# A two-layer fp32 trunk on one core: other places and turns for weights, a norm's root ahead of its queue, later dots, and one halved output at the end

## The chip, the cores and the metric

The kernel runs on one core of a Trainium2 chip. The metric is the device time of one execution in microseconds (us); the value of a kernel is the median of its runs.

## What is computed

The input is x with 512 tokens of 1024 features and a vector c; all numbers are fp32. Two layers follow each other, each with a mixer and an MLP, and each of the four parts begins with a norm whose scale, shift and gate come from c:

```python
for layer in range(2):
    mod = silu(c) @ ada_w[layer] + ada_b[layer]
    shift1, scale1, gate1, shift2, scale2, gate2 = split(mod, 6)
    h = rms_norm(x, norm_mix[layer]) * (1 + scale1) + shift1
    x = x + gate1 * mixer(h)          # layer 0: convolution and HGRN2; layer 1: stick-breaking attention
    h = rms_norm(x, norm_mlp[layer]) * (1 + scale2) + shift2
    x = x + gate2 * (square(relu(h @ w1[layer])) @ w2[layer])
```

## The kernel before

**Products.** TensorE (PE) holds a 128x128 piece of a weight and streams 512 or 256 tokens past it. For fp32 accuracy each weight and each activation is split into a high half and a rest, and `mm3` issues three matmuls for a product: L281 (high weight, high activation), L282 (high weight, low activation), L283 (low weight, high activation). A tile of weights is 128x1024. Its way is: a load from memory by SyncE's queue (L260, tile `wraw`, a ring of three), a cast on ScalarE (ACT) that makes the high half (L271, `whi`), a subtraction on VectorE (DVE) that makes the rest (L272, `wlo`). `whi` and `wlo` are rings of four, so a cast waits until PE has finished with the tile four turns earlier; a tile can also be given a place of its own (`of`), outside the ring. Tiles of the graph (below) go the same way with L1370, L1372 and L1373.

**Layer 0.** The functions are called in program order, and each engine takes its instructions in that order. The out projection (`proj`) makes eight outputs; outputs 4 to 7 (`HALVED`) are computed in two halves of 256 tokens, first half first, and `PLACES` says which of them have a weight place of their own. After each output `x_add` (L505) adds it to x, and the norm sums squares (`nsq`, `nss`). When a half is complete, L496 on PE sums over features, ACT and DVE make the root (`na`, `ny`), and per feature tile DVE makes `tt` (L465), ACT `hh` (L466) and DVE `hl` (L467). Then the MLP: `mlp_head` makes four hidden tiles half by half with the weights w1[0] to w1[3]; two whole tiles follow (w1[4], w1[5]); all others come in pairs by a Strassen-like scheme (`pair`), which needs sums of activations (`sums`, tiles t0 to t3) and of weights (`pair_w`). Four blocks `b` of eight hidden tiles each are multiplied with w2 (`second`, `products`). The function `rest()` is the end of a block's last pair: its hidden tile is split into `hidh` (L290, ACT) and `hidl` (L291, DVE), and the next product waits for it.

**Dots.** The 96 products of c with the weights of scale, shift and gate of both layers are done on DVE, 80 of them in `background(n)`: each loads 128x1024 weights into the same raw ring and multiplies and sums them (L419). `PIECES[b][o]` says how many stand behind output o of block b.

**Layer 1.** Up to its MLP's first four hidden tiles it is a graph of operations that a planner orders: each operation has an engine, a cost, what it reads and writes, and a priority (the number behind the lists in `on_act` and `on_dve`; the lower number goes first among those that are ready). PE's order is partly fixed as a chain. `finish` (L1400 to L1421) is the graph's norm: L1406 sums on PE, L1409 and L1410 make the logarithm and the exponential on ACT, L1411 to L1413 polish the root on DVE, and L1417, L1419 and L1421 make `tt`, `hh` and `hl` per feature tile. Attention begins with queries and keys of the first heads, whose squares (`nsq`, L1433 and L1450) PE sums by L1459. After the graph `mlp(1, True, ...)` runs in program order on PE, with the other engines in the same way, and at the end the outputs that are left are computed half by half, added to x and stored.

Of the kernel before, what the change touches and what calls it, by code (L numbers as in the profile page):

```python
# [13 lines left out]
F32 = mybir.dt.float32  # L14
# [5 lines left out]
AF = mybir.ActivationFunctionType  # L20
ALU = mybir.AluOpType
# [5 lines left out]
EPS = 1e-6  # L27
# [193 lines left out]
def trunk(tc, x_d, c_d, rep_d, small_d, const_d, ada_d, ws_d, win_d, wv_d, woab_d, w1_d, w2_d, wqk_d, wvc_d, woc_d, out_d):  # L221
# [30 lines left out]
    H = halves()  # L252
# [251 lines left out]
    def x_add(o, ps, sl, l, v):  # L504
        dve.scalar_tensor_tensor(x[o][:, sl], ps, mcol(l, v, o), x[o][:, sl], op0=ALU.mult, op1=ALU.add)  # L505
# [463 lines left out]
            nrm.add(o, sl)  # L969

    HALVED = (4, 5, 6, 7)
    PLACES = {5: (mp, "F2", "Q2"), 6: (mp, "Ft", "Kt")}
    w = [load_w(woab_d[o]) for o in (0, 1, 2)]
    background(2)
    run(proj((0, 1, 2), w, FULL))
# [161 lines left out]

    PIECES = ((2, 2, 3, 2, 2, 2), (2, 2, 3, 2, 2, 2), (2, 2, 2, 2, 2, 2), (2, 2, 2, 2, 2))  # L1140

    def mlp(l, last, hp, head, th, more=()):

        nrm = Norm(1, 0, (7,)) if not last else None
        ahead = None
        for b in range(4):
            hid, rest = list(head) if b == 0 else [], lambda: None
            if b == 0:
                for n, j in enumerate((4, 5)):
                    whole_tile(more[n] if more else load_w(w1_d[l, j]), j, hp, hid)  # L1150
            for i in range(len(hid) // 2, 4):
                rest = pair(4 * b + i, hp, th, hid, rest, ahead or pair_w(l, 4 * b + i, hp))
                ahead = None
            n = 8 if b < 3 else 5
            second = lambda o: (acc(), load_w(w2_d[l, b // 2, o, b % 2], None, AT256 if o == n - 1 else AT512))

            def products(p, k0, k1):
                for k in range(k0, k1):
                    mm3(p[0], p[1], ks(k), hid[k], FULL, k == 0, k == 7)

            def done(o, ps):
                x_add(o, ps, FULL, l, GATE2)
                if b == 3:
                    if last:
                        sync.dma_start(out_d[o], x[o])
                    else:
                        nrm.add(o, FULL)
                if 0 < o < len(PIECES[b]):
                    background(PIECES[b][o])

            p0 = second(0)
            products(p0, 0, 7)
            rest()
            background(PIECES[b][0])
            p1 = second(1)
            products(p1, 0, 7)
            for o, p in enumerate((p0, p1)):
                products(p, 7, 8)
                done(o, p[0])
            for o in range(2, n):  # L1180
                p = p1 if o == n - 1 and b < 3 else second(o)
                if o == n - 2 and b < 3:

                    p1, ahead = second(n - 1), pair_w(l, 4 * b + 4, hp)
                    next(ahead)
                    next(ahead)
                products(p, 0, 8)
                done(o, p[0])
# [12 lines left out]
        return nrm, ps, banks, hid, ws

    def mlp_head(l, nin, hp):
# [109 lines left out]
    def on_act(n, fn, r, w, prio=1, psum=False, column=False, **kw):  # L1313
        return G.op("ACT", act_us(n, psum, column), fn, r, w, prio, **kw)

    def on_dve(n, fn, r, w, prio=1, **kw):
        return G.op("DVE", dve_us(n), fn, r, w, prio, **kw)
# [83 lines left out]
    def finish(parts, hf, l, which, table, after=()):  # L1401

        sl, ps, a, y = H[hf], miscs.new(), nass.new(), nys.new()

        for i, q in enumerate(parts):
            on_pe(0.44, lambda i=i, q=q: pe.matmul(ps.t[:, :256], ones, q.t[:, sl], start=(i == 0), stop=(i == len(parts) - 1)),  # L1406
                  (q,), (ps,), 0, after=after if i == 0 else ())
        m = lambda: ps.t[:, :256]
        on_act(256, lambda: act.activation(a.t, m(), AF.Ln, scale=LS, bias=eps_b), (ps,), (a,), 0, psum=True, column=True, after=table)  # L1409
        on_act(256, lambda: act.activation(y.t, a.t, AF.Exp, scale=-0.5, bias=ls_b), (a,), (y,), 0, column=True)  # L1410
        on_dve(256, lambda: dve.scalar_tensor_tensor(a.t, m(), EPS, y.t, op0=ALU.add, op1=ALU.mult), (ps, y), (a,), 0)  # L1411
        on_dve(256, lambda: dve.tensor_tensor(a.t, a.t, y.t, op=ALU.mult), (y, a), (a,), 0)
        on_dve(256, lambda: dve.scalar_tensor_tensor(y.t, a.t, -3.0, y.t, op0=ALU.add, op1=ALU.mult), (a, y), (y,), 0)  # L1413
        for i in range(NT):
            t_, g, sh = tth[i][hf], l * 16 + which * 8 + i, mcol(l, SHIFT1 if which == 0 else SHIFT2, i)
            hi, lo = hh[hf][i]
            on_dve(310, lambda i=i, t_=t_, g=g: dve.scalar_tensor_tensor(t_.t[:, sl], x[i][:, sl], gsc[:, g:g + 1], y.t,  # L1417
                   op0=ALU.mult, op1=ALU.mult), (xh[i, hf], y), (t_,), 0)
            on_act(256, lambda t_=t_, sh=sh, hi=hi: act.activation(hi.t[:, sl], t_.t[:, sl], AF.Identity, bias=sh), (t_,), (hi,), 0,  # L1419
                   column=True)  # L1420
            on_dve(310, lambda t_=t_, sh=sh, hi=hi, lo=lo: dve.scalar_tensor_tensor(lo.t[:, sl], t_.t[:, sl], sh,  # L1421
                   hi.t[:, sl].bitcast(F32), op0=ALU.add, op1=ALU.subtract), (t_, hi), (lo,), 0)


    QQ, KK, kraw, sqs, rq, oT, vs = {}, {}, {}, {}, {}, {}, {}
# [277 lines left out]
    for hf, sl in enumerate(H):  # L1703
        if hf:
            finish([nt_.acc[1]] + [nt_.sq[o, 1] for o in nt_.direct], 1, 1, 1, (), [order[at + 8]])

        ps = [accs.new() for _ in range(2)] if hf == 0 else [zts.new() for _ in range(4)]
        ps = [(ps[j // 2], lambda t_, j=j: t_[:, H[j % 2]]) if hf == 0 else (ps[j], half) for j in range(4)]

        for k, j in by_half(0, 4) if hf == 0 else [(k, j) for js in ((0, 1), (2, 3)) for k in range(NT) for j in js]:  # L1710
            order.append(mm3h(*ps[j], w[j], ks(k), (hh[hf][k],), sl, k == 0 and (hf == 1 or j % 2 == 0), k == NT - 1, 256))
        for j in range(4):
            c_, (hi, lo), (p_, cut) = cms.new(), hid[j], ps[j]
            on_act(256, lambda c_=c_, p_=p_, cut=cut, sl=sl: act.activation(c_.t[:, sl], cut(p_.t), AF.Relu), (p_,), (c_,), 0, psum=True)
# [9 lines left out]
    order_s.close()  # L1724
    order_s.enter_context(tc.manual_schedule(engines={mybir.EngineType.PE}))

    _, ps, _, hk, ws = mlp(1, True, h1, [(a.t, b.t) for a, b in hid], [(a.t, b.t) for a, b in th])
    for hf in range(2):
        for o in range(5, 8):
            for k in range(8):  # L1730
                mm3(ps[o, hf], ws[o - 5], ks(k), hk[k], H[hf], k == 0, k == 7)
            x_add(o, ps[o, hf], H[hf], 1, GATE2)
            sync.dma_start(out_d[o][:, H[hf]], x[o][:, H[hf]])
    order_s.close()
    m_s1.close()
    es.close()
# [69 lines left out]
```

## Time and profile before

| What | Value |
|---|---|
| median of 3 runs | 1243.63 us (1243.44, 1243.63, 1245.4) |
| the profiled execution | 1245.21 us, its span 1243.4 us |
| TensorE busy | 1217.4 us, 98% of the span |
| TensorE weight load busy | 1058.9 us, 85% |
| VectorE busy | 890.5 us, 72% |
| ScalarE busy | 618.7 us, 50% |
| mean granted TensorE clock | 0.996 of 2.4 GHz |

The span is the time between the first and the last instruction of the profiled execution; 1.8 us of that execution lie around it. An engine is busy while it executes an instruction; TensorE's matmuls overlap, so that its busy time holds their pipeline too. In the views below a time such as 268.60 is counted from the span's start, and a bracket at a row's end gives the idle time of that engine just before, with what ended it.

### The profile page before, as it was taken

How to read it: one execution, taken by the hardware profiler on the slowest of the kernel's cores; microseconds unless marked ns; L12 is line 12 of the kernel's file. 1: busy time of each engine (PE TensorE's matmuls, PEld its weight loads, DVE VectorE, ACT ScalarE, POOL GpSimd, SP SyncE). 2: the span in 40 equal slices, each digit the busy share in tenths (PEclk: the TensorE clock that was granted, in tenths of full speed). 3: DMA queues.
4: the chain of work that ended last, by engine and by line, in shares of the span. 5: the costliest groups of instructions: out<-in, count | busy, mean ns of one | idle time of the engine just before them, and what ended most of it. 6: DMA issues, size and time to landing. Idle time of an engine off the chain costs nothing.

```text
span 1243.4 us, 19173 instructions
## 1 busy us (share of the span) xinstructions
PE 1217.4 (98%) x7649; PEld 1058.9 (85%) x7649; DVE 890.5 (72%) x1435; ACT 618.7 (50%) x1111; POOL 11.2 (1%) x24
## 2 busy tenths in 40 slices
PE   7999999989999999999999999999989999999998
PEld 6888877889899899898977877787878898998998
DVE  8996868769788687787857765568694585665761
ACT  4433233347256265274568655667465283472650
POOL 0000000000000000000300000000000000000000
PEclk9999999999999999999999999999999999999999
DMA  8764444623745727527332122323114223143141
GB/s 305 258 208 161 143 153 135 203 69 107 246 135 183 245 92 244 179 99 259 110 102 85 52 68 85 94 60 103 35 37 134 85 101 122 58 146 102 54 151 51
DMA packets 46618, 163.50 MB, mean 131 GB/s; under 512 B 5296, under 2 KB 6328, under 8 KB 46528
## 3 DMA queue, kind: packets, MB, share of 16 engines
q1 hardware_dynamic: 46384, 161.78, 39.5%
q8 instruction: 60, 0.98, 0.3%
q10 hardware_dynamic: 144, 0.49, 0.1%
q14 instruction: 30, 0.25, 0.1%
HBM read 155.96 MB, written 2.10 MB: 127 GB/s over the span
## 4 chain that ended last, share of the span: by engine, by line
PE 84%; DVE 8%; DMA 4%; ACT 2%; issue 1%; SPq 0%; DVEq 0%; ACTq 0%
PE b L281 20%; PE b L283 20%; PE b L282 20%; PE acc L281 3%; PE acc L283 3%; PE acc L282 3%; PE b L1539 2%; PE b L1560 1%; DMA raw<-in_ws 1%; PE b L1595 1%; PE b L1459 1%; DMA wraw<-in_w 1%; PE b L1596 1%; PE b L1597 1%; DVE wlo L272 1%
## 5 line engine op out<-in xcount | busy, mean ns | idle before, releaser
L271 ACT CAST whi<-wraw 128x1024 fp32r<-128x1024 f32 x125 | 130.0, 1048 | 217.9 <-DMA wraw<-in_w 87.7
L282 PE MATMUL b<-hidl,whi 128*128 128x512 f32 (+1 forms) x560 | 208.4, 372 | 1.0 <-DVE hidl L291 1.0
L281 PE MATMUL b<-hidh,whi 128*128 128x512 f32 (+1 forms) x560 | 208.6, 373 | 0.2
L283 PE MATMUL b<-hidh,wlo 128*128 128x512 f32 (+1 forms) x560 | 208.0, 371 | 0.0
L283 PE MATMUL b<-hh,wlo 128*128 128x256 f32 (+1 forms) x632 | 193.5, 306 | 7.1 <-DVE wlo L272 7.1
L281 PE MATMUL b<-hh,whi 128*128 128x256 f32 (+1 forms) x632 | 197.6, 313 | 2.0 <-ACT hh L1419 2.0
L282 PE MATMUL b<-hl,whi 128*128 128x256 f32 (+1 forms) x632 | 193.3, 306 | 1.2 <-DVE hl L1421 1.2
L272 DVE TENSOR_TENSOR wlo<-wraw,whi 128x1024 fp32r<-128x1024 f32 x125 | 152.1, 1222 | 58.8 <-ACT whi L271 57.6
L281 PEld LDWEIGHTS b<-hh,whi 128*128 128x128 f32 x632 | 120.4, 191 | 14.6 <-issue 7.2
L283 PEld LDWEIGHTS b<-hh,wlo 128*128 128x128 f32 x632 | 120.5, 191 | 13.3 <-DVE wlo L272 7.8
L282 PEld LDWEIGHTS b<-hl,whi 128*128 128x128 f32 x632 | 121.8, 193 | 6.2 <-DVE hl L1421 1.8
L282 PEld LDWEIGHTS b<-hidl,whi 128*128 128x128 f32 x560 | 105.6, 188 | 19.5 <-DVE hidl L291 1.6
L505 DVE SCALAR_TENSOR_TENSOR x<-b,modc,x 128x512 f32<-128x512 f32 (+1 forms) x102 | 68.2, 675 | 75.2 <-PE b L283 75.1
L281 PEld LDWEIGHTS b<-hidh,whi 128*128 128x128 f32 x560 | 105.2, 188 | 19.1 <-ACT hidh L290 1.0
L283 PEld LDWEIGHTS b<-hidh,wlo 128*128 128x128 f32 x560 | 105.2, 188 | 18.5
L419 DVE CUSTOM_DVE_ANT_0 wraw<-wraw,cb 128x1024 f32<-128x1024 f32 x80 | 97.4, 1221 | 26.3 <-DMA wraw<-in_ada 25.9
L272 DVE TENSOR_TENSOR wlo<-tt,whi 128x1024 fp32r<-128x1024 f32 x52 | 63.4, 1221 | 22.5 <-ACT whi L271 21.9
L271 ACT CAST whi<-tt 128x1024 fp32r<-128x1024 f32 x52 | 53.4, 1049 | 45.3 <-PE b L282 32.7
L1373 DVE TENSOR_TENSOR wlo<-raw,whi 128x1024 fp32r<-128x1024 f32 x34 | 41.6, 1222 | 23.6 <-ACT whi L1372 23.5
L291 DVE TENSOR_TENSOR hidl<-cm,hidh 128x256 fp32r<-128x256 f32 (+1 forms) x90 | 44.4, 510 | 18.5 <-ACT hidh L290 17.7
L281 PE MATMUL acc<-hh,whi 128*128 128x512 f32 x128 | 52.3, 408 | 0.0
L1523 DVE TENSOR_TENSOR_SCAN om<-om,pat 128x772 f32<-128x772 f32 (+2 forms) x24 | 46.5, 1936 | 5.8 <-ACT om L1519 5.8
(378 smaller groups left out, 2631.4 us busy)
## 6 DMA issues: line engine op xcount, KB each, us to landing
wraw<-in_w SPq DMA_DIRECT2D x124, 512.0 KB, 3.6
wraw<-in_ada SPq DMA_DIRECT2D x80, 512.0 KB, 4.3
eraw<-in_ada SPq DMA_DIRECT2D x16, 512.0 KB, 3.7
wraw<-in_win SPq DMA_DIRECT2D x16, 512.0 KB, 3.5
raw<-in_wqk SPq DMA_DIRECT2D x16, 512.0 KB, 4.1
raw<-in_ws SPq DMA_DIRECT2D x8, 512.0 KB, 6.0
wraw<-in_woab SPq DMA_DIRECT2D x8, 512.0 KB, 3.2
raw<-in_wvc SPq DMA_DIRECT2D x8, 512.0 KB, 3.3
```

Source lines behind the costliest of these rows:

```text
L271: act.copy(hi, raw)
L272: dve.tensor_tensor(lo, raw, hi.bitcast(F32), op=ALU.subtract)
L281: pe.matmul(ps, whi, h[0][:, hs], start=start, stop=False, **kw)
L282: pe.matmul(ps, whi, h[1][:, hs], start=False, stop=False, **kw)
L283: pe.matmul(ps, wlo, h[0][:, hs], start=False, stop=stop, **kw)
L291: dve.tensor_tensor(lo[:, sl], t_[:, sl], hi[:, sl].bitcast(F32), op=ALU.subtract)
L419: dve.tensor_tensor_reduce(out=raw, in0=raw, in1=cb, scale=1.0, scalar=0.0, op0=ALU.mult, op1=ALU.add, accum_out=modr[:, col:col + 1])
L505: dve.scalar_tensor_tensor(x[o][:, sl], ps, mcol(l, v, o), x[o][:, sl], op0=ALU.mult, op1=ALU.add)
L1373: on_dve(1024, lambda: dve.tensor_tensor(lo.t, raw.t, hi.t.bitcast(F32), op=ALU.subtract), (raw, hi), (lo,), 1)
L1459: on_pe(0.13, lambda s=s, sq=sqs[p, s, s0]: pe.matmul(ms.t[64 + 32 * s:96 + 32 * s, sl], hs, sq.t[:, sl], start=True, stop=True), (sqs[p, ...
L1523: on_dve(2 * nw, lambda: dve.tensor_tensor_scan(s_(), s_(), pats[i][:, ::-1], 0.0, op0=ALU.mult, op1=ALU.max), (om,), (om,), 2)
L1539: pe.transpose(tp.t[:, o_:o_ + P], be.t[:, w0:w0 + P], ident)
```

## The change

- The out projection's outputs 6 and 7, and no longer 5 and 6, have weight places of their own.
- Behind output 0 of a block the dots no longer stand between `rest()` and `second(1)` but behind the output's end, like all others; the count behind output 0 is now 0, and the others take more.
- In the graph's norm the root's operations have priority -1 instead of 0, and `tt`, `hh`, `hl` of the second half of the tokens (`hf` is 1) have -1 too.
- The two whole tiles' weights of layer 1's MLP, w1[4] and w1[5], are loaded and split inside the graph, before the sums.
- At the end of layer 1 only output 7 is halved; outputs 5 and 6 are computed with 512 tokens like the others.

```diff
-    PLACES = {5: (mp, "F2", "Q2"), 6: (mp, "Ft", "Kt")}
+    PLACES = {6: (mp, "F2", "Q2"), 7: (mp, "Ft", "Kt")}
...
-    PIECES = ((2, 2, 3, 2, 2, 2), (2, 2, 3, 2, 2, 2), (2, 2, 2, 2, 2, 2), (2, 2, 2, 2, 2))
+    PIECES = ((0, 2, 3, 3, 3, 2), (0, 2, 3, 3, 3, 2), (0, 2, 3, 3, 2, 2), (0, 2, 3, 3, 2))
...
-            n = 8 if b < 3 else 5
+            n = 8 if b < 3 else 7 if last else 5
...
-                if 0 < o < len(PIECES[b]):
+                if o < len(PIECES[b]):
                     background(PIECES[b][o])
...
             rest()
-            background(PIECES[b][0])
             p1 = second(1)
...
-        on_act(256, lambda: act.activation(a.t, m(), AF.Ln, scale=LS, bias=eps_b), (ps,), (a,), 0, psum=True, column=True, after=table)
-        on_act(256, lambda: act.activation(y.t, a.t, AF.Exp, scale=-0.5, bias=ls_b), (a,), (y,), 0, column=True)
+        on_act(256, lambda: act.activation(a.t, m(), AF.Ln, scale=LS, bias=eps_b), (ps,), (a,), -1, psum=True, column=True, after=table)
+        on_act(256, lambda: act.activation(y.t, a.t, AF.Exp, scale=-0.5, bias=ls_b), (a,), (y,), -1, column=True)
...
             on_dve(310, lambda i=i, t_=t_, g=g: dve.scalar_tensor_tensor(t_.t[:, sl], x[i][:, sl], gsc[:, g:g + 1], y.t,
-                   op0=ALU.mult, op1=ALU.mult), (xh[i, hf], y), (t_,), 0)
+                   op0=ALU.mult, op1=ALU.mult), (xh[i, hf], y), (t_,), -hf)
...
+    more = [weights(w1_d[1, j]) for j in (4, 5)]
     sums(1, th, issue)
...
-    _, ps, _, hk, ws = mlp(1, True, h1, [(a.t, b.t) for a, b in hid], [(a.t, b.t) for a, b in th])
+    _, ps, _, hk, ws = mlp(1, True, h1, [(a.t, b.t) for a, b in hid], [(a.t, b.t) for a, b in th], [(a.t, b.t) for a, b in more])
...
-        for o in range(5, 8):
-            for k in range(8):
-                mm3(ps[o, hf], ws[o - 5], ks(k), hk[k], H[hf], k == 0, k == 7)
-            x_add(o, ps[o, hf], H[hf], 1, GATE2)
-            sync.dma_start(out_d[o][:, H[hf]], x[o][:, H[hf]])
+        for k in range(8):
+            mm3(ps[7, hf], ws[0], ks(k), hk[k], H[hf], k == 0, k == 7)
+        x_add(7, ps[7, hf], H[hf], 1, GATE2)
+        sync.dma_start(out_d[7][:, H[hf]], x[7][:, H[hf]])
```

PE's own order is the same in both kernels but for two places: the end, which has 48 matmuls fewer, and the start of layer 1's attention, where one L1459 stands three matmuls earlier. What moves is on the other engines, at three places.

**Place 1: DVE at the end of layer 0's out projection**, as a piece of the difference. `ny` is the root of the first half's norm, `tt` belongs to that norm, and `wlo` is the low half of w1[3].

```order
 L505 SCALAR_TENSOR_TENSOR x_66<-acc,modc,x_66 128x256
 L336 SCALAR_TENSOR_TENSOR ny<-na,ny 128x256
+L272 TENSOR_TENSOR wlo<-wraw,whi 128x1024
 L465 SCALAR_TENSOR_TENSOR tt<-x_61,gsc,ny 128x256
 L465 SCALAR_TENSOR_TENSOR tt<-x_62,gsc,ny 128x256
```

The same instruction stood before behind the eight `tt`, the eight `hl` and the last addition to x; it is now ahead of them, and its cast on ACT, too, stands ahead of the first `hh`.

**Place 2: ACT at the start of layer 1's attention**, the order of the change. `nsq<-b_5879` and `nsq<-b_5891` are the squares of the first two heads' queries, `nsq<-b_5884` those of the first keys, and `hh` is the norm's high half for the second half of the tokens.

```order
L1433 ACTIVATE nsq<-b_5879 128x256
L1419 ACTIVATE hh_5628<-tt,modc 128x256
L1419 ACTIVATE hh_5630<-tt,modc 128x256
L1419 ACTIVATE hh_5632<-tt,modc 128x256
L1419 ACTIVATE hh_5634<-tt,modc 128x256
L1437 CAST stq<-b_5879 64x256 x2
L1449 COPY kraw<-b_5884 128x256
L1450 ACTIVATE nsq<-b_5884 128x256
L1433 ACTIVATE nsq<-b_5891 128x256
```

Before, the four `hh` stood behind all the squares of the first two heads; on PE the three L1459 that read the squares of the first queries, the first keys and the second queries now stand in a row.

**Place 3: DVE at the end of the graph**, first before, then in the change. `t0l` to `t3l` are the low halves of the sums, L1717 makes `hidl` of the first four hidden tiles, and the first two of the three `wlo` belong to w1[4] and w1[5].

```order
L1026 TENSOR_TENSOR t0l<-tt,t0h 128x1024
L1033 SCALAR_TENSOR_TENSOR tt<-tt,modc 128x256 x5
L1717 TENSOR_TENSOR hidl_8954<-cm,hidh_8939 128x256
L1717 TENSOR_TENSOR hidl_8960<-cm,hidh_8944 128x256
L1033 SCALAR_TENSOR_TENSOR tt<-tt,modc 128x256 x3
L1026 TENSOR_TENSOR t1l<-tt,t1h 128x1024
L1026 TENSOR_TENSOR t2l<-tt,t2h 128x1024
L1026 TENSOR_TENSOR t3l<-tt,t3h 128x1024
L1717 TENSOR_TENSOR hidl_8981<-cm,hidh_8972 128x256
L1717 TENSOR_TENSOR hidl_8993<-cm,hidh_8983 128x256
L272 TENSOR_TENSOR wlo<-wraw,whi 128x1024 x3
```

```order
L1033 SCALAR_TENSOR_TENSOR tt<-tt,modc 128x256 x2
L1372 TENSOR_TENSOR wlo<-raw,whi 128x1024
L1033 SCALAR_TENSOR_TENSOR tt<-tt,modc 128x256
L1717 TENSOR_TENSOR hidl_8979<-cm,hidh_8966 128x256
L1372 TENSOR_TENSOR wlo<-raw,whi 128x1024
L1033 SCALAR_TENSOR_TENSOR tt<-tt,modc 128x256 x3
L272 TENSOR_TENSOR wlo<-wraw,whi 128x1024
L1717 TENSOR_TENSOR hidl_9012<-cm,hidh_8994 128x256
L1717 TENSOR_TENSOR hidl_9039<-cm,hidh_9025 128x256
L1033 SCALAR_TENSOR_TENSOR tt<-tt,modc 128x256 x2
L1026 TENSOR_TENSOR t1l<-tt,t1h 128x1024
L1026 TENSOR_TENSOR t2l<-tt,t2h 128x1024
```

All three `wlo` now stand ahead of `t1l` to `t3l`. A little earlier on DVE, three `hl` of the norm (L1421) have moved ahead of the sums' first subtraction (L1036), behind which they stood.

## Rows read from the trace of the kernel before

**Rows 1.** The page: busy times, a group of instructions, a kind of load.

```profile
PE 1217.4 (98%) x7649; PEld 1058.9 (85%) x7649; DVE 890.5 (72%) x1435; ACT 618.7 (50%) x1111; POOL 11.2 (1%) x24
...
L419 DVE CUSTOM_DVE_ANT_0 wraw<-wraw,cb 128x1024 f32<-128x1024 f32 x80 | 97.4, 1221 | 26.3 <-DMA wraw<-in_ada 25.9
...
wraw<-in_w SPq DMA_DIRECT2D x124, 512.0 KB, 3.6
```

**Rows 2.** Waits of PE over the span: total us, times, longest.

```profile
PE b L283 <- DVE wlo L272: 7.1, 2, 4.0
...
PE b L281 <- ACT hh L1419: 2.0, 1, 2.0
```

**Rows 3.** Timeline of PE around 268 us: start, us, instruction, idle before.

```profile
268.60 0.57 PE L283 MATMUL b<-hh,wlo 128*128 128x256 f32 x1 [3.19 <-DVE wlo L272]
...
271.52 0.86 PE L496 MATMUL b<-nss,ones 128*128 128x256 f32 x2
```

**Rows 4.** Timeline of PE, 889 to 925 us.

```profile
891.92 0.38 PE L281 MATMUL b<-hh,whi 128*128 128x256 f32 x1 [1.97 <-ACT hh L1419]
...
912.11 0.39 PE L282 MATMUL b<-hl,whi 128*128 128x256 f32 x1 [0.52 <-DVE hl L1421]
...
923.56 0.50 PE L283 MATMUL b<-hh,wlo 128*128 128x512 f32 x1 [3.96 <-DVE wlo L272]
```

**Rows 5.** Windows: length, busy us (x instructions) of PE, PEld, DVE, ACT, POOL, then granted clock, DMA.

```profile
893.28:896.70 3.42, 3.42 (x18) 3.42 (x17) 3.42 (x10) 1.71 (x4) 0.00 (x0) 0.50 0.00 0
924.00:927.42 3.42, 3.42 (x10) 2.67 (x9) 1.77 (x2) 0.00 (x0) 0.00 (x0) 0.50 0.69 216
...
268.64:272.06 3.42, 3.42 (x15) 3.33 (x16) 0.00 (x0) 0.00 (x0) 0.00 (x0) 0.50 0.46 153
```

**Rows 6.** Timeline of DVE, 259 to 269 us.

```profile
259.07 0.41 DVE L336 SCALAR_TENSOR_TENSOR ny<-na,ny 128x256 f32<-128x256 f32 x1
...
266.94 0.47 DVE L505 SCALAR_TENSOR_TENSOR x<-acc,modc,x 128x256 f32<-128x256 f32 x1
267.33 1.21 DVE L272 TENSOR_TENSOR wlo<-wraw,whi 128x1024 fp32r<-128x1024 f32 x1
```

**Rows 7.** Timeline of ACT, 263 to 268 us.

```profile
263.81 1.05 ACT L271 CAST whi<-wraw 128x1024 fp32r<-128x1024 f32 x1
...
267.50 0.42 ACT L485 ACTIVATE nsq<-x 128x256 f32<-128x256 f32 x1 [1.10 <-DVE x L505]
```

**Rows 8.** Timeline of PE in layer 0's MLP, last block.

```profile
567.51 0.50 PE L282 MATMUL b<-hidl,whi 128*128 128x512 f32 x1 [0.74 <-DVE hidl L291]
```

**Rows 9.** Timeline of ACT at the start of layer 1's attention.

```profile
622.50 0.39 ACT L1450 ACTIVATE nsq<-b 128x256 f32<-128x256 f32 x1
...
624.63 1.30 ACT L1419 ACTIVATE hh<-tt,modc 128x256 fp32r<-128x256 f32 x3
```

**Rows 10.** Timeline of PE at the start of layer 1's attention.

```profile
622.95 0.62 PE L1459 MATMUL b<-nsq,cons 128*32 128x256 f32 x2 [0.22 <-ACT nsq L1450]
```

**Rows 11.** Timeline of DVE, 889 to 935 us.

```profile
889.99 0.48 DVE L505 SCALAR_TENSOR_TENSOR x<-b,modc,x 128x256 f32<-128x256 f32 x1 [0.20 <-PE b L283]
890.39 0.41 DVE L1413 SCALAR_TENSOR_TENSOR ny<-na,ny 128x256 f32<-128x256 f32 x1
...
920.48 1.22 DVE L1026 TENSOR_TENSOR t3l<-tt,t3h 128x1024 fp32r<-128x1024 f32 x1
...
922.28 3.49 DVE L272 TENSOR_TENSOR wlo<-wraw,whi 128x1024 fp32r<-128x1024 f32 x3
928.74 0.69 DVE L1065 TENSOR_TENSOR tt<-wraw 128x512 f32<-128x512 f32 x1 [2.97 <-DMA wraw<-in_w]
...
931.76 2.49 DVE L272 TENSOR_TENSOR wlo<-tt,whi 128x1024 fp32r<-128x1024 f32 x2
```

**Rows 12.** Windows of PE alone at 512 and at 256 tokens: length, busy us (x matmuls), clock, DMA.

```profile
1203.00:1213.00 10.00, 10.00 (x45) 1.00 0.31 107
1228.00:1238.00 10.00, 10.00 (x87) 1.00 0.13 42
```

More of the change, by code (lines that the diff above doesn't have):

```diff
@@ L1194, in mlp @@
         ps, banks, ws = {}, {}, []
-        for o in range(5, 8):
+        for o in range(n, 8):
             for hf in range(2):
@@ L1198, in mlp @@
                 ps[o, hf] = acc(256)
-            ws.append(load_w(w2_d[l, 1, o, 1], None if o == 5 else (hp, f"t{o - 6}h", f"t{o - 6}l"), AT256))
+            ws.append(load_w(w2_d[l, 1, o, 1], None if o == n else (hp, f"t{o - 6}h", f"t{o - 6}l"), AT256))
         return nrm, ps, banks, hid, ws
@@ L1408, in finish @@
         m = lambda: ps.t[:, :256]
-        on_act(256, lambda: act.activation(a.t, m(), AF.Ln, scale=LS, bias=eps_b), (ps,), (a,), 0, psum=True, column=True, after=table)
-        on_act(256, lambda: act.activation(y.t, a.t, AF.Exp, scale=-0.5, bias=ls_b), (a,), (y,), 0, column=True)
-        on_dve(256, lambda: dve.scalar_tensor_tensor(a.t, m(), EPS, y.t, op0=ALU.add, op1=ALU.mult), (ps, y), (a,), 0)
-        on_dve(256, lambda: dve.tensor_tensor(a.t, a.t, y.t, op=ALU.mult), (y, a), (a,), 0)
-        on_dve(256, lambda: dve.scalar_tensor_tensor(y.t, a.t, -3.0, y.t, op0=ALU.add, op1=ALU.mult), (a, y), (y,), 0)
+        on_act(256, lambda: act.activation(a.t, m(), AF.Ln, scale=LS, bias=eps_b), (ps,), (a,), -1, psum=True, column=True, after=table)
+        on_act(256, lambda: act.activation(y.t, a.t, AF.Exp, scale=-0.5, bias=ls_b), (a,), (y,), -1, column=True)
+        on_dve(256, lambda: dve.scalar_tensor_tensor(a.t, m(), EPS, y.t, op0=ALU.add, op1=ALU.mult), (ps, y), (a,), -1)
+        on_dve(256, lambda: dve.tensor_tensor(a.t, a.t, y.t, op=ALU.mult), (y, a), (a,), -1)
+        on_dve(256, lambda: dve.scalar_tensor_tensor(y.t, a.t, -3.0, y.t, op0=ALU.add, op1=ALU.mult), (a, y), (y,), -1)
         for i in range(NT):
@@ L1417, in finish @@
             on_dve(310, lambda i=i, t_=t_, g=g: dve.scalar_tensor_tensor(t_.t[:, sl], x[i][:, sl], gsc[:, g:g + 1], y.t,
-                   op0=ALU.mult, op1=ALU.mult), (xh[i, hf], y), (t_,), 0)
-            on_act(256, lambda t_=t_, sh=sh, hi=hi: act.activation(hi.t[:, sl], t_.t[:, sl], AF.Identity, bias=sh), (t_,), (hi,), 0,
+                   op0=ALU.mult, op1=ALU.mult), (xh[i, hf], y), (t_,), -hf)
+            on_act(256, lambda t_=t_, sh=sh, hi=hi: act.activation(hi.t[:, sl], t_.t[:, sl], AF.Identity, bias=sh), (t_,), (hi,), -hf,
                    column=True)
             on_dve(310, lambda t_=t_, sh=sh, hi=hi, lo=lo: dve.scalar_tensor_tensor(lo.t[:, sl], t_.t[:, sl], sh,
-                   hi.t[:, sl].bitcast(F32), op0=ALU.add, op1=ALU.subtract), (t_, hi), (lo,), 0)
+                   hi.t[:, sl].bitcast(F32), op0=ALU.add, op1=ALU.subtract), (t_, hi), (lo,), -hf)
     QQ, KK, kraw, sqs, rq, oT, vs = {}, {}, {}, {}, {}, {}, {}
@@ L1725, in trunk @@
     order_s.enter_context(tc.manual_schedule(engines={mybir.EngineType.PE}))
-    _, ps, _, hk, ws = mlp(1, True, h1, [(a.t, b.t) for a, b in hid], [(a.t, b.t) for a, b in th])
+    _, ps, _, hk, ws = mlp(1, True, h1, [(a.t, b.t) for a, b in hid], [(a.t, b.t) for a, b in th], [(a.t, b.t) for a, b in more])
     for hf in range(2):
-        for o in range(5, 8):
-            for k in range(8):
-                mm3(ps[o, hf], ws[o - 5], ks(k), hk[k], H[hf], k == 0, k == 7)
-            x_add(o, ps[o, hf], H[hf], 1, GATE2)
-            sync.dma_start(out_d[o][:, H[hf]], x[o][:, H[hf]])
+        for k in range(8):
+            mm3(ps[7, hf], ws[0], ks(k), hk[k], H[hf], k == 0, k == 7)
+        x_add(7, ps[7, hf], H[hf], 1, GATE2)
+        sync.dma_start(out_d[7][:, H[hf]], x[7][:, H[hf]])
     order_s.close()
```

## The prediction

> **What bounds the kernel now.** I read the page first, for the engine that sets the time, then the waits of that engine, then the timelines around each wait. The page shows TensorE (PE) busy for 1217.4 of 1243.4 us [rows 1]: the reader is to see that nothing but PE's own work, its clock and its few stops can move the time by much. The list of waits gives the stops that this change touches: 7.1 us in two waits for the low half of a weight tile, 2.0 us in one wait for the norm's `hh` [rows 2]. The timelines put them at three places: 265.4 to 268.6 us [rows 3], 889.9 to 912.1 us, and 919.6 to 923.6 us [rows 4].
>
> The third thing to see is the clock. In three stretches of 3.42 us the granted clock was 0.50, which is 1.2 of 2.4 GHz [rows 5]; each begins at or just after one of these stops. At half clock 3.42 us do the work of 1.71 us, so such a stretch costs another 1.7 us. The stops and their stretches together cost about 3.2 + 2.0 + 0.5 + 4.0 + 3 x 1.7 = 14.8 us, the most that the change can win apart from the tail.
>
> **A. Weight places of the out projection.** PE stops at 265.4 us for the low half of w1[3] until 268.60, then issues 13 matmuls and reaches L496 at 271.52 [rows 3]. That low half stands last on DVE (267.33 to 268.54) behind the eight `tt`, the eight `hl` and the last addition [rows 6]; its cast started only at 263.81 [rows 7], when a ring slot that output 7 held came free. In the change it takes output 5's slot, which is free some 6 us earlier, and its low half follows `ny`, so from about 259.5 [rows 6]. It is then ready 5 us before PE asks. But everything behind it on DVE moves back by one such subtraction less its overlap, 1.14 us: the last additions to x end at about 268.2, and the square and the sum that L496 reads (one on ACT 0.42 us [rows 7], one on DVE) follow by about 268.7. PE does its 13 matmuls at full clock in half of 2.9 us, arrives near 266.8 and now waits 1.9 us for the norm. L496 at 268.7 instead of 271.52 is 2.8 us earlier; the rest of the half-clock stretch behind 271.52 (0.5 us) adds 0.25. I take **-3.0**, if the clock stays up after this shorter wait, and -1.3 if it falls again. No wait at all would be -5.0; nothing allows that, since the norm's inputs are late.
>
> **B. Dots behind later outputs.** The number of dots in a block stays (13, 13, 12, 10), each 1.22 us of DVE [rows 1]. Taken out from behind `rest()`, they let the next weight tile, w2's third, be loaded and split earlier; its cast and its subtraction (1.21 us [rows 6]) now stand ahead of the last `hidh` and `hidl`, which PE waits for. In the last block PE already waits 0.74 us for `hidl` [rows 8], in the first about 0.4, in the two between the rest ends just in time. Where the subtraction takes the place of a dot nothing is lost, where it is added up to 1.2 us. I take 0.7 gained in the first block, 0.3 in the last, and 0.25 lost in each of the two others: **-0.5**, with -1.4 (all such waits gone) and +2.5 as bounds. The later outputs get one more dot each; their weights are ready at least 1.5 us early, so DVE's slack there covers it; without that cover it would be 1.2 us for each of the up to three outputs that get one.
>
> **C. Layer 1's first norm.** ACT takes four `hh` (three last 1.30 us, so four about 1.7 [rows 9]) between the first queries' square and the copies behind it. The first keys' square, at 622.50 before [rows 9], comes about 1.6 us later, near 624.1. PE's L1459 that reads it started at 622.95, after a wait of 0.22 [rows 10]; it will start near 624.5. This is a new wait: **+1.55**. Queued behind it on PE are the second queries' L1459 and the products of the second half, whose `hh` and `hl` are now ready earlier, so nothing adds to it. Bounds: +1.0 if the `hh` start before the square is due, +3.3 if the clock falls.
>
> **D. Layer 1's second norm and the whole tiles.** Three terms. First, the wait of 1.97 us for `hh` [rows 4]: `tt` needs the last addition to x (889.99) and `ny` (890.39) [rows 11]; the addition is PE's own last output and doesn't move, only the 0.41 us of `ny` go ahead of it: **-0.45**. Second, the wait of 0.52 for `hl` [rows 4], where `hl` stood behind a 1.2 us subtraction of the sums: **-0.5**. Third, the wait of 3.96 us for w1[4]'s low half [rows 4]: the three `wlo` started at 922.28, behind `t3l` and its like [rows 11]. In the change w1[4]'s stands five operations behind `t0l`, about 915.5 to 916.6, and w1[5]'s ends near 918.5; PE asks at 919.4 less the 1 us gained above. The stop goes, and with it the stretch of half clock that follows: -4.0 - 1.7 = **-5.7**. What is late next is the first pair's weight sum: its four steps began at 928.74 after a load, and its low half at 931.76 [rows 11]. PE reaches it 5.7 us earlier, by my count at about 930.6; DVE has 3.4 us of `wlo` ahead of `t3l` instead of behind, and is done with the sum's first low half near 931.2: **+0.6**, between 0 and 1.6.
>
> **E. The end.** 96 matmuls of 256 tokens become 48 of 512. In 10 us PE issues 87 of the one and 45 of the other [rows 12], 0.115 and 0.222 us each (those lapping the edges counted in both), so 48 x (2 x 0.115 - 0.222) = **-0.4**, between 0.3 and 0.5. The last addition and store keep their size.
>
> **The sum** is -3.0 - 0.5 + 1.55 - 0.45 - 0.5 - 5.7 + 0.6 - 0.4 = -8.4 us against the profiled execution's 1245.2 (span 1243.4 and 1.8 around it): 1236.8. The median of the runs shown is 1.6 lower, one of the three runs 1.8 above the other two. I read that gap as one stretch of half clock that not every run has, which the trace can't tell. If it is one that the change removes, the median gains only 6.7 (1236.9); if not, the median goes to 1235.2. I take 1236.2.
>
> **A rule against this sum.** After a wait of 1.97 us the clock fell [rows 4, 5], so waits near 2 us, as the new ones of A and C, may cost 1.7 us more each. The Trainium skill, page "TensorE: Matmul & The Clock Gate", section "HAM oscillation — how this bites in real kernels", says that only idle gaps beyond a certain length must be avoided; by it the new waits, being shorter than any that it names, would leave the clock up and the sum would be -8.4. By the row it is -5.0 if both trip. The trace differs from the page there: 1.97 us was enough once, with 0.7 more shortly behind.
>
> **The rivals.** *The waits only change places.* A's new wait for the norm and C's for the squares each bring a half-clock stretch, and the pair's sum is late by 1.6: -8.4 + 1.7 + 1.7 + 1.0 = -4.0, about 1240.5. For it speaks the clock's fall after 1.97 us; against it that many waits of under 1 us had none. *All goes well*: the clock also stays up after D's first wait, shortened to 1.5 (-1.7), the pair's sum is in time (-0.6) and no block's `hidl` is late (-0.9): 1233. *Slower, by one mechanism:* the third w2 tile's load is issued behind a dot and its cast stands ahead of `hidh` on ACT. If it lands late, ACT and with it PE wait in all four blocks of layer 0, each up to a load's 3.6 us [rows 1]: -8.4 + 4 x 3.6 = +6.0, 1249.6. It decides from 2.8 us a block on. Against it: the load is due some microseconds before. *The change doesn't do what it says:* w1[3]'s slot is freed no earlier, and A gives nothing: -5.4, 1239.
>
> **How the numbers follow.** A measurement of this kernel can tell about 0.2% from no change, 2.5 us. The forecast, with its own spread of 1234 to 1238.5, has 0.58; waits that only change places 0.19; all going well 0.07; A alone without effect 0.05; slower by the loads 0.06; losses that just cancel the gain 0.05. The first, third and fourth are faster by over 2.5 us, and three quarters of the second: 0.84. Of the rest 0.10 is within 0.2% and 0.06 slower. The range of 1231.5 to 1242 takes in the first four cases but for their edges, some 0.82; its low end is A to D with every bound on the good side, its high end the first rival with B's loss.
>
> **What would show it.** Right: no wait for `wlo` L272 in PE's list; a wait of about 2 us before L496 near 267 us; a wait of about 1.5 us at L1459 near 623; the stretch of 0.50 behind 924 gone; 48 fewer matmuls. Wrong: L496 waiting over 3 us, `hidl` waits of over 2 us in each block, a stop of some microseconds at the first pair of layer 1, or more than two stretches at half clock.

## The result, and the profile after

The changed kernel takes 1238.04 us (median of 5 runs, 1237.66 to 1238.95); beside it four runs of the kernel before took 1243.44 to 1245.4, and a fifth, slow one took 1717.87 and is left out. The ratio is 0.9946 (0.9932 to 0.9959): 6.7 us faster (5.1 to 8.5). The profiled execution has a span of 1237.2 us against 1243.4. The prediction was 1236.2 with a range of 1231.5 to 1242; the time lies inside, 1.8 above.

The page of the changed kernel, its first part, which answers to the first of [rows 1]:

```profile
PE 1213.8 (98%) x7601; PEld 1054.9 (85%) x7601; DVE 889.8 (72%) x1433; ACT 618.5 (50%) x1111; POOL 11.2 (1%) x24
```

PE has 48 matmuls fewer (7649 before) and is busy for 98% of the span as before. Its waits (total, times, longest) answer to [rows 2]:

```profile
PE b L496 <- DVE nss L490: 2.4, 1, 2.4
PE b L282 <- DVE hidl L291: 2.1, 4, 1.1
...
PE b L1459 <- ACT nsq L1450: 1.8, 1, 1.8
PE b L281 <- ACT hh L1419: 1.5, 1, 1.5
...
PE b L282 <- DVE hl L1421: 0.7, 1, 0.7
PE b L283 <- DVE wlo L272: 0.3, 1, 0.3
```

The 7.1 us of waits for low halves are 0.3 now. In their place stand a wait of 2.4 for the norm at L496 (forecast 1.9), of 1.8 at L1459 (forecast about 1.6 more than 0.2), and 2.1 in four waits for `hidl`. The kernel before had two of those:

```profile
PE b L282 <- DVE hidl L291: 1.0, 2, 0.7
```

The windows of the changed kernel (columns as in [rows 5]) behind four stops, L496, L1459, the wait for `hh`, and the place where w1[4]'s low half was late:

```profile
270.00:273.40 3.40, 3.40 (x25) 3.30 (x26) 1.15 (x3) 0.98 (x2) 0.00 (x0) 1.00 0.02 5
624.50:627.90 3.40, 3.40 (x21) 2.11 (x21) 1.11 (x4) 1.71 (x6) 0.00 (x0) 1.00 0.00 0
893.40:896.80 3.40, 3.26 (x15) 3.26 (x16) 3.40 (x10) 1.94 (x5) 0.00 (x0) 0.52 0.00 0
919.90:923.30 3.40, 3.40 (x16) 2.81 (x16) 3.40 (x7) 3.22 (x8) 0.00 (x0) 1.00 0.48 159
```

Of the three stretches at half clock [rows 5] one is left, the one behind the wait for `hh`. This execution has another from 19.5 to 22.9 us, where the kernel before had none; nothing of the change reaches there.

**A ledger.** To see where the time went I took the same instruction in each trace (by line and turn) and subtracted its start in the kernel before. What this difference gains between two such places is that segment's. The places are the last L798 of layer 0's mixer (PE), the first `kept` of a pair (a product that ACT copies, L1098), the last one of layer 0, the first and last L1539 of attention (PE), the first and last `kept` of layer 1, and PE's last matmul, with their times in the kernel before. In us, minus is faster; e1 to e11 are runs told of below:

| Segment before | changed | e1 | e2 | e3 | e4 | e9 | e10 | e11 |
|---|---|---|---|---|---|---|---|---|
| 0 to 161.6 | +0.93 | +0.27 | +0.46 | -0.93 | -0.44 | +1.12 | +0.50 | +1.50 |
| to 304.7 (A) | -1.92 | +0.72 | -1.35 | -2.97 | -1.34 | -0.72 | -1.35 | -1.40 |
| to 558.1 (B, three blocks) | +1.72 | +1.31 | +0.05 | +1.16 | +1.12 | +0.60 | +1.02 | +0.68 |
| to 657.5 (B's last block, C) | +0.32 | +1.78 | -0.23 | -0.49 | +0.94 | -1.22 | -0.53 | +1.66 |
| to 869.6 (attention) | -0.02 | -0.02 | -0.07 | -0.04 | -0.06 | -0.18 | -0.01 | 0.00 |
| to 937.8 (D) | -6.74 | -6.59 | -6.25 | -7.42 | -6.20 | -6.59 | -1.62 | -6.68 |
| to 1190.2 | 0.00 | -0.24 | -0.24 | 0.00 | -0.41 | -0.23 | 0.00 | -0.24 |
| to 1239.8 (E) | -0.43 | -0.43 | -0.43 | -0.43 | -0.43 | -0.43 | -0.43 | 0.00 |

The first row is a measure of scatter: no part of the change reaches there, and the segment differs by 2.4 us between executions.

### The profile page after: what moved, and what is told of

Same layout as the page of the kernel before. It is cut to its first block, busy times and chain, and to the rows that moved or that the text cites. A ratio compares the mean times of both kernels' runs of the same rounds, so it can differ in the third digit from the quotient of the medians.

```text
span 1237.2 us, 19078 instructions
## 1 busy us (share of the span) xinstructions
PE 1213.8 (98%) x7601; PEld 1054.9 (85%) x7601; DVE 889.8 (72%) x1433; ACT 618.5 (50%) x1111; POOL 11.2 (1%) x24
## 4 chain that ended last, share of the span: by engine, by line
PE 77%; DVE 10%; DMA 7%; ACT 4%; issue 2%; SPq 0%; ACTq 0%; DVEq 0%
PE b L281 19%; PE b L282 19%; PE b L283 19%; DMA wraw<-in_ada 2%; DMA raw<-in_ws 2%; DVE wlo L272 2%; PE acc L281 2%; PE acc L282 2%; PE acc L283 2%; PE b L1539 2%; PE b L1560 1%; DMA wraw<-in_w 1%; PE b L1595 1%; ACT whi L271 1%; PE b L1459 1%
## 5 line engine op out<-in xcount | busy, mean ns | idle before, releaser
L282 PE MATMUL b<-hidl,whi 128*128 128x512 f32 (+1 forms) x544 | 205.8, 378 | 2.1 <-DVE hidl L291 2.1
L281 PE MATMUL b<-hidh,whi 128*128 128x512 f32 (+1 forms) x544 | 205.5, 378 | 0.0
L283 PE MATMUL b<-hidh,wlo 128*128 128x512 f32 (+1 forms) x544 | 205.1, 377 | 0.0
L282 PEld LDWEIGHTS b<-hidl,whi 128*128 128x128 f32 x544 | 102.4, 188 | 22.3 <-DVE hidl L291 3.8
L283 PEld LDWEIGHTS b<-hidh,wlo 128*128 128x128 f32 x544 | 102.2, 188 | 19.2 <-DVE wlo L272 0.2
L281 PEld LDWEIGHTS b<-hidh,whi 128*128 128x128 f32 x544 | 102.1, 188 | 18.7
L291 DVE TENSOR_TENSOR hidl<-cm,hidh 128x256 fp32r<-128x256 f32 (+1 forms) x90 | 44.6, 512 | 20.6 <-ACT hidh L290 19.5
```

The costliest lines, as they stand in the source:

```text
L291: dve.tensor_tensor(lo[:, sl], t_[:, sl], hi[:, sl].bitcast(F32), op=ALU.subtract)
```

## The experiments

Each is the changed kernel but for its edit. Ratios are to the kernel before, beside which each ran; its median lay between 1244.1 and 1245.2 us, so that medians of different runs compare to about 1 us only.

**e1: the old weight places.**

```diff
-    PLACES = {6: (mp, "F2", "Q2"), 7: (mp, "Ft", "Kt")}
+    PLACES = {5: (mp, "F2", "Q2"), 6: (mp, "Ft", "Kt")}
```

> The changed kernel with the weight places of the out projection as before (outputs 5 and 6). Theory, from the two traces laid side by side: the places are worth 1.9 us, so this kernel is about 1.9 us slower than the changed one (near 1240.0); PE waits 3.2 us for the low half of w1[3] near 269 us, the clock falls behind it, the wait of 2.4 us before L496 is gone, and the matmuls of 256 tokens behind it are again 0.113 us apart instead of 0.118. Rival, the prediction's own term: 3.0 us slower (near 1241.0), with the same distance between matmuls in both.

Measured: 1240.15 us, ratio 0.9967 (0.9958 to 0.9977), 2.1 slower than the changed kernel. The waits of e1 in PE's list:

```profile
PE b L283 <- DVE wlo L272: 3.4, 2, 3.2
```

The wait for the low half is back, that of L496 is gone, and the clock was at half in the 3.4 us behind it:

```profile
268.90:272.30 3.40, 3.40 (x15) 3.31 (x16) 0.00 (x0) 0.00 (x0) 0.00 (x0) 0.51 0.50 154
```

The ledger's segment goes from -1.92 to +0.72, a difference of 2.6, between the two expectations. The 0.72 is not the places': here, with the code of before, the matmuls behind the stop were 0.118 us apart, and 0.113 before. So my theory was wrong in one point: the distance doesn't follow the places (below).

**e2: the old dots.** The table of before, and the first pieces again between `rest()` and `second(1)`.

```diff
-    PIECES = ((0, 2, 3, 3, 3, 2), (0, 2, 3, 3, 3, 2), (0, 2, 3, 3, 2, 2), (0, 2, 3, 3, 2))
+    PIECES = ((2, 2, 3, 2, 2, 2), (2, 2, 3, 2, 2, 2), (2, 2, 2, 2, 2, 2), (2, 2, 2, 2, 2))
...
             rest()
+            background(PIECES[b][0])
             p1 = second(1)
```

> The changed kernel with the dots of layer 0's MLP as before. Theory: the later dots cost 0.9 us, so this kernel is about 0.9 us faster than the changed one (near 1237.1); the four waits for the last hidl of a block go from 1.1, 0.3, 0.6, 0.3 back to about 0.2, 0, 0, 0.7. Rival, the prediction's term: the later dots gain 0.5, so this kernel is 0.5 us slower (near 1238.5).

Measured: 1236.92 us, ratio 0.9935 (0.9916 to 0.9954). The median is 1.1 below the changed kernel's, though the intervals overlap. PE's waits for `hidl` in e2:

```profile
PE b L282 <- DVE hidl L291: 0.5, 2, 0.3
```

The ledger doesn't settle it either. Over the three blocks the seven runs of the table with the later dots are 0.6 to 1.7 longer than before and e2 only 0.05; but e6, e7 and e12 (below), which have the old dots too and L496 later, are 0.9, 1.1 and 1.5 longer. One part stands out: from 387.8 to 461.2 us, where the outputs of the second block lie, all seven lose 0.45 to 1.65, and the four with the old dots lose 0.54, 0.08, 0.01 and 0.01. In the first block (to 358.8) the changed kernel's trace loses 0.47, but the other six gain 0.1 to 0.7. So the later dots probably cost time in the second block; that they cost any over the whole is not shown.

Where PE waits for `hidl` stands in the changed kernel's own timelines. DVE in block 0, then ACT in block 2:

```profile
311.68 0.42 DVE L1120 TENSOR_TENSOR cm<-b,kept 128x256 f32<-128x256 f32 x1
313.83 1.23 DVE L419 CUSTOM_DVE_ANT_0 wraw<-wraw,cb 128x1024 f32<-128x1024 f32 x1 [1.73 <-DMA wraw<-in_ada]
314.98 0.08 DVE L419 DVE_READ_ACCUMULATOR2_ANT modr<- 128x1 f32 x1
314.98 1.02 DVE L291 TENSOR_TENSOR hidl<-cm,hidh 128x512 fp32r<-128x512 f32 x2
```

```profile
479.11 0.63 ACT L1104 ACTIVATE cm<-cm 128x512 f32<-128x512 f32 x1
480.67 1.05 ACT L271 CAST whi<-wraw 128x1024 fp32r<-128x1024 f32 x1 [0.93 <-DMA wraw<-in_w]
481.62 0.61 ACT L290 CAST hidh<-cm 128x512 fp32r<-128x512 f32 x1
```

In block 0 a dot still stands ahead of `hidl`, and its weights come late: DVE idles 1.73 us and PE waits 1.1 behind it. In block 2 the third w2 tile's load comes late, and its cast holds `hidh` up for 0.93 + 1.05 us. PE waits 0.6 behind it. That is the mechanism of the prediction's slower rival, at a sixth of its price.

**e3: priority 0 in both norms of the graph** (all `-1` and `-hf` of the change are 0 again).

> The changed kernel with priority 0 in both norms of the graph. Theory: the first norm's priority costs 1.1 us (L1459 waits 1.8 us for the keys' squares; here 0.2), the second's gains 1.1 (here the waits for hh and hl are 0.5 and 0.5 longer), so the sum is within 0.3 us of the changed kernel (near 1238). Rival: the wait at L1459 is covered by slack behind it in attention, so only the second norm counts and this kernel is 1.1 us slower (near 1239.1).

Measured: 1238.43 us, ratio 0.9951 (0.9935 to 0.9968), near the theory's number; the interval, 1236.0 to 1240.1 us, holds the rival's as well. L1459 waits 0.2 again, and the waits for `hh` and `hl` are those of before. The profiled execution is 5 us shorter than the changed kernel's, and most of that has nothing to do with the priorities: 1.9 lie before 161.6 us, 1.1 in segment A and 0.6 in the three blocks. Its windows behind L496 and behind the wait for `hh`:

```profile
267.80:271.20 3.40, 3.40 (x26) 3.30 (x27) 1.12 (x3) 0.98 (x2) 0.00 (x0) 1.00 0.02 5
888.70:892.10 3.40, 2.74 (x22) 2.54 (x23) 3.40 (x10) 1.94 (x6) 0.00 (x0) 1.00 0.00 0
```

Here the clock stayed up behind the wait of 2.0 for `hh` (PE idle until 888.65), the same wait behind which it fell before; and segment A came to -2.97, the prediction's -3.0.

**e4: the whole tiles' weights behind the sums again.**

```diff
-    more = [weights(w1_d[1, j]) for j in (4, 5)]
...
-    _, ps, _, hk, ws = mlp(1, True, h1, [(a.t, b.t) for a, b in hid], [(a.t, b.t) for a, b in th], [(a.t, b.t) for a, b in more])
+    _, ps, _, hk, ws = mlp(1, True, h1, [(a.t, b.t) for a, b in hid], [(a.t, b.t) for a, b in th])
```

> The changed kernel with the two whole tiles' weights loaded behind the sums as before. Theory: PE waits about 4 us for w1[4]'s low half again and the clock falls behind it, 1.7 us more; the pair's wait of 0.4 goes: this kernel is 5 to 5.6 us slower (near 1243.4). Rival: with the norm's hl ahead, the sums and the low halves end earlier on DVE than before, the wait is shorter than 3 us and the clock stays up: 2.5 us slower (near 1240.5).

Measured: 1238.39 us, ratio 0.9956 (0.9939 to 0.9973): no difference beyond the scatter, and both expectations missed. PE doesn't wait for w1[4] here either. With the norm's priority alone, the scheduler puts its low half directly behind `t0l`; DVE in e4:

```profile
912.80 1.22 DVE L1026 TENSOR_TENSOR t0l<-tt,t0h 128x1024 fp32r<-128x1024 f32 x1
913.93 1.22 DVE L272 TENSOR_TENSOR wlo<-wraw,whi 128x1024 fp32r<-128x1024 f32 x1
```

So two parts each seem to remove the same wait; the run without both settles it.

**e10: priority 0 and the weights behind the sums** (the edits of e3 and e4).

> The changed kernel with priority 0 in both norms and the whole tiles' weights behind the sums: both parts undone, each of which undone alone left no wait for w1[4]. Theory: either part alone lets its low half go ahead of the sums, so only without both does the wait of about 4 us come back, with a stretch of half clock behind it: 5 to 6 us slower than the changed kernel, near 1243.5. Rival: the wait went for another reason (the tail, the weight places, the dots, which move the loads), and it stays away here too: near 1238.

Measured: 1242.74 us, ratio 0.9978 (0.9969 to 0.9987), 4.7 slower than the changed kernel (4.0 by the two ratios), close to the theory. PE in e10, and the window behind:

```profile
921.59 0.79 PE L283 MATMUL b<-hh,wlo 128*128 128x512 f32 x1 [3.95 <-DVE wlo L272]
```

```profile
921.60:925.00 3.40, 3.40 (x8) 2.72 (x9) 2.20 (x2) 0.00 (x0) 0.00 (x0) 0.50 0.65 196
```

The wait of 3.95 and its half clock are those of before. With either part (e3 has the weights' load alone, e4 the priorities alone) they are gone.

**e9: raised priorities in the second norm alone** (`-1` becomes `-which`, `-hf` becomes `-hf * which`).

> The changed kernel with the raised priorities in the second norm of the graph alone. Theory: the first norm's priority is the whole cause of the wait at L1459 (1.8 us) and the second norm's of the gains at 890 to 912 us; this kernel is 0.8 to 1.1 us faster than the changed one where the segment up to attention ends, near 1237.0, with D's gains kept. Rival: the two can't be parted, since the planner's order of the attention shifts with the first; the second norm's gain is lost, near 1238.

Measured: 1236.3 us, ratio 0.9925 (0.9904 to 0.9946), an interval that holds both expectations. The segments decide: the one to attention is 1.5 shorter than in the changed kernel, D keeps its -6.6, and L1459 waits 0.2:

```profile
PE b L1459 <- ACT nsq L1450: 0.2, 1, 0.2
```

The first norm's priority is a pure cost.

**e11: three halved outputs at the end** (the loop of before over outputs 5 to 7).

> The changed kernel with three halved outputs at the end as before. Theory: 48 products of 512 tokens become 96 of 256: the segment from the last pair of layer 1 to the last matmul is 0.4 us longer, all else as in the changed kernel. Rival: the shorter last additions and stores of halved outputs bring the end forward by as much, and the difference is below 0.1.

Measured: one run, 1240.7 us. Its last segment is 0.00 against -0.43 in every other run of the table, and the end follows the last matmul by 0.09 more than in them: E is worth 0.52 us.

**e5: L496 later.** The wait left by A is for late inputs, so other work should stand in front of it:

```diff
-        later(TN, lambda: nin.finish(acc(256), 1))
+        later(4.4, lambda: nin.finish(acc(256), 1))
```

> The changed kernel with the sums of the second half's norm (L496) 24 matmuls later in PE's order (the delay in the MLP's head 4.4 instead of 2). Theory: the wait that the weight places left is one for the norm's late inputs, so work in front of L496 fills it: no wait there, from the last L498 of attention's layer to the first pair 2.2 to 2.5 us shorter, near 1235.6. Rival: the second half's hh and hl are then late by the same time, PE waits for them behind the first half, and nothing is gained (near 1238).

Measured: 1238.92 us, ratio 0.9951 (0.9936 to 0.9965). The wait at L496 is gone and segment A comes to -3.12, but the median is no better. In the profiled execution, the slowest of four, the clock was at half for 6.8 us behind L1459, and the three blocks cost +4.78: a new wait in block 0's later outputs, at half clock from 339 to 342:

```profile
PE b L281 <- ACT whi L271: 1.9, 1, 1.9
```

ACT's cast ran at 337.3, when the load had landed; SP had issued that load only at 331.9, behind three loads of dots that shared the ring with it, and it took over 5 us beside others. The prediction's "at least 1.5 us early" for the later outputs doesn't hold here.

**e6: joined**: the edits of e5, e2 and e9 at once.

> The changed kernel with three parts altered at once: L496 later as in the run with the later norm, the dots as before, and the priorities in the second norm of the graph alone. Theory, from the ledger of segments: -2.3 for L496, -1.3 for the dots, -0.9 for the wait at L1459, so near 1233.5. Rival: part of these is scatter of loads and clock between runs, and the sum comes to half, near 1235.8.

Measured: 1233.43 us (1231.47 to 1236.1), ratio 0.9908 (0.9894 to 0.9923): 4.6 us faster than the changed kernel and 11.5 than before, at the theory's number. It has the lowest median here. That the number fits so well is in part luck: against the changed kernel's segments A gains 1.6 (the theory had 2.3), the three blocks 0.85 (1.3) and the next segment 1.7 (0.9), and the rival's 1235.8 lies within the runs. Its segments against before: A -3.54, the three blocks +0.87, the next -1.36, D -8.20; the last is so large because the profiled execution, the fastest of five, has no stretch at half clock at all. PE's remaining waits that the change speaks of (line numbers are one higher here):

```profile
PE b L281 <- ACT hh L1420: 1.5, 1, 1.5
PE b L283 <- DVE wlo L272: 1.2, 3, 0.5
...
PE b L282 <- DVE hl L1422: 0.7, 1, 0.7
...
PE b L1460 <- ACT nsq L1451: 0.2, 1, 0.2
```

**e7 and e12: also the first half of the second norm.** e7 is e6 with `-which` for `tt`, `hh` and `hl` of both halves; e12 raises `tt` and `hh` of the first half's first four tiles only.

> The joined kernel with the priority of tt, hh and hl raised for both halves of the second norm. Theory: the two waits of 1.5 and 0.7 us near 892 us go, since tt need not stand behind the last additions to x; with them the stretch of half clock: 2 to 3.5 us faster than the joined kernel. Rival: the sixteen tt and hl ahead of the last three additions make the second half's squares 5 us later, and PE waits for them at the sums of that half: no gain, or 1 us slower.

> The joined kernel with the priority of tt and hh of the first four tiles of the first half raised as well (not hl), so that they go ahead of the last three additions to x, and the squares are late by 1.6 us only. Theory: the wait of 1.5 us for hh near 887 us goes, one of about 1 us for hl stays in place of 0.7; 1.2 to 1.6 us faster than the joined kernel, near 1232. Rival: the last additions hold PE's banks or the sums of the second half up, and it is no faster (near 1233.4).

Measured: e7 1236.07, ratio 0.9928 (0.9913 to 0.9944); e12 1235.19, ratio 0.9916 (0.99 to 0.9933). Neither beats e6. In e7 the wait for `hh` goes, but PE waits 0.6 for `hl`, and 0.9 and 0.8 at the first pair, with a stretch at half clock behind; in e12 the wait turns into one for `hl`, behind the additions that went first. PE in e12:

```profile
890.55 0.39 PE L282 MATMUL b<-hl,whi 128*128 128x256 f32 x1 [2.43 <-DVE hl L1422]
```

It is as long as the two of e6 together (2.2). In both orders tried the waits changed places and did not go; that DVE's whole row of additions, `tt` and `hl` is what PE waits for is a reading that no run shows.

**e8: another first column for each pair's weights** (one of 0, 8, 16, 24, 32, 40, 48 and 64), about the two distances between matmuls.

> The changed kernel with another first column for the weights of each pair of hidden tiles in the MLPs (0, 8, 16, 24, 32, 40, 48, 64 in turn; all 16 in the changed kernel), to see the distance between matmuls of 256 tokens pair by pair. It is 0.118 us in all pairs and 0.113 in some other stretches. Theory: the first column decides, and some columns give 0.113 or other values in both layers alike. Rival: the distance is set at the last stop of PE, whatever the column; then all pairs show 0.118.

Measured: one run, 1239.53 us. Neither: the distance depends on the column, alike in both layers, but nearly all of them give 0.117 to 0.120 us. Only the weights of a pair's last product (tiles of their own, computed inside the next pair) give 0.113, at column 48, while the three other weights of the same pair at 48 give 0.118. The 16 of the kernel is among the best.

## Why the prediction was right, and where it wasn't

**What bounds it**: right in the main. PE's stops and clock make 4.2 of the 6.2 us between the two executions and E's shorter work 0.4. The rest lies in the distances between PE's matmuls, which the prediction took as fixed and which change (below).

**A, -3.0 forecast, -1.92 measured.** The mechanism is as told: PE takes up w1[3] with no wait and stops at L496 instead. PE in the changed kernel:

```profile
267.26 0.28 PE L283 MATMUL b<-hh,wlo 128*128 128x256 f32 x1
269.97 0.70 PE L496 MATMUL b<-nss,ones 128*128 128x256 f32 x2 [2.43 <-DVE nss L490]
```

Allowing for the 0.93 of a later start, L496 is at 269.0 (forecast 268.7). The clock stayed up here and in e3 and e8, which have this code too, and fell in e2, e4, e9, e10 and e11. Both branches of the forecast are borne out: -3.0 if the clock stays up (-2.97 in e3), -1.3 if it falls (-1.33 to -1.40 in e2, e4, e10 and e11). The step that failed is the one that priced the work behind the stop as unchanged: before, the 160 matmuls from 272 to 291 us stood 0.113 us apart, here 0.118, which takes 0.7 us back. Over seven of these eight traces (all but e8's) the segment ranges from -0.7 to -3.0, clock and distance making the difference.

**B, -0.5 forecast, a loss measured in this trace, its cause open.** The three blocks lost 1.72 here and 0.6 to 1.3 in the other six traces of the table with the later dots. The last block (558.1 us to the first L1459) gained 0.2 to 1.2 in all seven, but 0.4 to 1.4 with the old dots (e2, e6, e7, e12) too. All four blocks together come to +0.90 here, -0.6 to +0.9 in the seven, -1.3 to +1.0 in the four with the old dots: the gain of 0.5 is not borne out, and a loss by the dots is not shown beyond scatter (e2). The working had two faults. It took "0.7 gained in the first block" from a wait that it put at about 0.4 and that is 0.23 in the trace of before. And it counted DVE's time in front of `hidl` and took the loads as punctual, though the trace of before has a weight's cast that waits for its load there (ACT at 399.87 us, 0.93 us). Also, the text ahead of the prediction says that every engine takes its instructions in program order. In layer 0, as in layer 1's MLP, only PE does, and the framework's scheduler orders DVE, ACT and SP; so a dot can stand ahead of `hidl` although the code puts it behind.

**C, +1.55 forecast.** L1459 waits 1.8 us as forecast, and its start is 1.6 us later than the products just before it. Behind it PE makes up 0.5, since the next L1459 already stands ahead of three matmuls; from 626 us on the difference is 1.1. From the first L1459 to 657.5 us the loss is 1.14 in the changed kernel, e2 and e4, 2.6 and 2.7 in e1 and e11, where the clock fell behind the wait, and at most 0.16 in the runs without the priority. So the wait is as forecast; the forecast took all of it to the segment's end, and 1.1 arrive there.

**D, -6.05 forecast, -6.74 measured.** The wait for `hh` went from 1.97 to 1.5, that of 0.52 for `hl` went, that of 3.96 with its half clock went, and the first pair waits 0.3: four steps as forecast, which come to -6.4; where the other 0.4 lies is open. But the prediction gave the third to the weights' earlier load. e4 shows that this is not needed, and e3, e4 and e10 together that the priorities or the load suffice alone. DVE of the changed kernel, w1[4]'s low half where it was forecast (915.5):

```profile
915.82 1.23 DVE L1372 TENSOR_TENSOR wlo<-raw,whi 128x1024 fp32r<-128x1024 f32 x1
```

**E, -0.4 forecast, -0.43 measured**, and 0.09 at the end.

Together: forecast -8.4, measured -6.2 between the two profiled executions; of the difference of 2.2, the later start makes 0.9, A 1.1, B and C together 1.0, and D and E give 0.8 back. That the sum came out so near is in part luck, since the errors are as large as the scatter between executions.

**The rule weighed against the sum.** Of the two readings the row's was the better one: waits of about 2 us can bring the clock down. What neither said is that they do so in some executions and not in others. The Trainium skill, page "TensorE: Matmul & The Clock Gate", section "What's actually happening", says that the window over which PE's activity is judged runs freely and doesn't start anew with the kernel; the scatter below agrees with that, and no run here tests it.

**The rivals.** Waits that only change places happened in part (L496, L1459, four `hidl`). The loads that come late are real: PE waits 0.2 to 0.6 us for the cast of the third w2 tile in three blocks, and 1.1 in the first for a dot's load, where the rival had up to 3.6 in each.

## What to carry to other kernels

When two edits could each remove the same wait, make a run with both undone: here either one was enough, so undoing one alone showed nothing. Three things together gave 4.6 us more than the change itself: work put in front of a stop (L496 later), a priority raised only where it is needed, and the dots back in their old places; the first alone showed no gain. Loads that share a queue with the weights should be counted as late ones, not as free slots on the engine that reads them.

## What the runs showed of the hardware

**Behind waits of about 2 us the clock falls in some executions and not in others.** In twelve traces (e7 and e12 aside) the granted clock was at 0.50 behind the wait at L496 (2.0 to 2.4 us) in 5 of 8, behind L1459 (1.8) in 3 of 7, behind the waits for `hh` and `hl` (1.5 to 2.0 and 0.7) in 7 of 12, and behind the waits of over 3 us for a low half in all 4. Windows of e10 behind L496 and of e1 behind L1459, where the changed kernel has 1.00:

```profile
269.60:273.00 3.40, 3.40 (x15) 3.12 (x14) 0.93 (x3) 0.98 (x2) 0.00 (x0) 0.51 0.00 0
```

```profile
627.30:630.70 3.40, 3.40 (x15) 2.37 (x13) 0.62 (x3) 0.53 (x2) 0.00 (x0) 0.51 0.00 0
```

This is not limited to the places of the change: near 17 us, where all fourteen traces have a wait of 1.8 to 3.2 us for `hh` (L651, in e8 L653), the clock fell behind it in nine. In e7 waits of 0.9 and 0.8 us close together were followed by it, in e12 one of 2.4 was not. A stretch costs up to 1.7 us (1.4 and 1.6 more in e1 and e11 at L1459). That is part of why a kernel's runs differ by several us (e3's median is 1238.43, its runs go from 1233.97 to 1239.86), but not all: e5's run with a mean clock of 0.994 took 1236.62 us, and one with 0.999 took 1239.21.

**The same matmuls run at two distances with the clock at 1.00.** The windows of PE alone (length, busy us and matmuls, clock) of the kernel before and of the changed one, in the same stretch of products of 256 tokens:

```profile
275.00:285.00 10.00, 10.00 (x90) 1.00 0.00 0
```

```profile
275.00:285.00 10.00, 10.00 (x87) 1.00 0.00 0
```

The distance is constant in these stretches between two stops and can change at one: at the stop near 268 us it went from 0.118 to 0.113 in before, e2, e3, e4, e8, e10 and e11, from 0.113 to 0.118 in the changed kernel, and stayed at 0.118 in e1 and e9. Most products of 256 tokens of the MLPs run at 0.118. What decides is open; e8 shows that the column of the weights has a part in it.
